# Expert weights in 8 KB rows and two experts per pass in the first expert stage of a two-block transformer kernel

## The chip, the cores and the metric

The kernel runs on one core of a Trainium2 chip (trn2). Its time is the device time of one execution in microseconds; the number that counts is the median of several executions. The core has TensorE (PE in the rows, with its weight loads as PEld), VectorE (DVE), ScalarE (ACT), GpSimd (POOL) and SyncE (SP), which here issues all DMAs; 16 DMA engines serve the core. TensorE's clock has two levels, 1.2 and 2.4 GHz; the profile shows the granted clock as a share of the higher one.

## The reference, cut to what matters

A first block (attention and feed-forward layers) is followed by a second block of two layers. Each of those two has attention branches and then a mixture of experts with 16 experts. In layer 0 the mixture runs over two streams of 256 tokens (`x` and the context), in layer 1 over `x` alone. Each expert takes the 32 tokens of a stream that score best for it, so 64 tokens in layer 0 and 32 in layer 1.

```python
def ec_moe(h, w_r, w1, w3, w2):
    B, n, D = h.shape
    cap = max(1, EC_CAPACITY * n // N_EXPERTS)          # 32
    aff = jax.nn.softmax((h @ w_r).astype(jnp.float32), axis=-1)
    gate, idx = lax.top_k(jnp.swapaxes(aff, 1, 2), cap)
    xin = jax.vmap(lambda hb, ib: hb[ib])(h, idx)
    hid = jax.nn.silu(jnp.einsum('becd,edf->becf', xin, w1)) * jnp.einsum('becd,edf->becf', xin, w3)
    ye = jnp.einsum('becf,efd->becd', hid, w2) * gate[..., None].astype(h.dtype)
    return jax.vmap(lambda yb, ib: jnp.zeros((n, D), h.dtype).at[ib.reshape(-1)].add(yb.reshape(-1, D)))(ye, idx)
```

Each of w1, w3 and w2 is 1024 x 1024 in fp32 for every expert, 12 MiB per expert and 192 MiB per layer.

## The kernel before

The program is written in the order of the model; a scheduler then orders the instructions of each engine, and pools of tiles set which buffer an instruction waits for. The expert part is the function `moe` (line 1540), called for layer 0 with two streams (`ns` = 2; "stage 0" below) and for layer 1 with one (`ns` = 1; "stage 1").

**Weights.** `ld` (line 1573) loads 256 rows of an expert's matrix, 1 MiB, into one tile of 8 KB per partition with `Ring.load` (lines 131 to 136). Partition p gets rows p and p + 128 of the 256, two runs of 4 KB. A `Ring` is a list of tile pools taken in turn, each of one tile: 16 tiles in stage 0 (lines 1546 and 1547), 19 in stage 1 (lines 1549 to 1551). A load waits on SP until the products that read the tile's last contents are done. SP issues DMAs in its own order, one after the other; what stands behind a waiting load waits too. Many of the ring's tiles lie where the attention part of the same layer had its buffers, so they come free as that part ends.

**First products** (`first_product`, lines 1576 to 1589). The gathered tokens `xin` are the stationary operand, the weights are the moving one, 512 columns at a time. In stage 0 the stationary operand has 64 columns, half of the array. Line 1585 multiplies by w1 into partitions 0 to 63 of a bank, line 1586 by w3 into partitions 64 to 127; the two run side by side. One expert takes two banks.

**Hidden layer and second products.** `gated` (line 1630) forms silu(a) * b on ScalarE and VectorE. `second_product` (line 1639) transposes it (line 1646), copies it to `hT` (line 1648) and multiplies by w2 (line 1655). With 64 tokens the contraction over 1024 is cut in two: the upper half of it goes to partitions 0 to 63 of `y`, the lower half to partitions 64 to 127, and the two are added by the scatter. The last expert's w2 comes in four slices of 256 columns, which have runs of 1 KB.

**Scatter.** For each quarter of the 1024 columns line 1686 scales `y` by the gate, lines 378 and 379 split it in two fp32r parts, lines 1693 and 1694 multiply a one-hot matrix `Se` by them for every 128 tokens, and line 1696 adds the result to the residual stream (`xr`, `xc`). This is done once per expert. In program order expert e's second products and scatter stand between the two halves of expert e + 1's first products.

**Start of a stage.** `u_gather` (line 1020) multiplies the normalised tokens by a one-hot matrix `G` to make `xin`, 128 features at a time, with the first expert's first products between. PSUM has eight banks, all from one pool.

Of the kernel before, what the change touches and what calls it, by code (L numbers as in the profile page):

```python
# [10 lines left out]
F32 = mybir.dt.float32  # L11
# [58 lines left out]
def model(ctx, tc, I, out):  # L70
# [6 lines left out]
    per = opool(ctx, "per")  # L77
    psum = opool(ctx, "psum", bufs=8, space=PSUM)
# [10 lines left out]
    def sub(hl, *ix):  # L89
        return hl[0][ix], hl[1][ix]  # L90

# [29 lines left out]
    class Ring:  # L121
# [9 lines left out]
        def load(self, src, k, c):  # L131
# [4 lines left out]
            return v  # L136

# [54 lines left out]
    pe.transpose(b[:, :128], rows, ident)  # L192
    dve.tensor_copy(cols, b[:, :128])

# [277 lines left out]
    def u_mod(ring, l, g):  # L472
# [22 lines left out]
        def fin():  # L495
# [3 lines left out]
            for q in range(4):  # L499
                pe.transpose(b2[:, q * 128:q * 128 + 128], mt[:, q * 128:q * 128 + 128], ident)  # L500
# [335 lines left out]
    for l in range(2):  # L836
        nc.sync.dma_start(WR[l], I["w_router_2"][l].rearrange("(k p) e -> p k e", p=128))
# [26 lines left out]
    def u_route(l, s, sp, half, pieces):  # L864
# [38 lines left out]
        def tr(t, i, on_act):  # L903
            def f():
# [4 lines left out]
                for k in range(c.start // 128, c.stop // 128):  # L909
                    pe.transpose(b[:, k * 128 - c.start:k * 128 - c.start + 128], X[s][:, t, k * 128:k * 128 + 128], ident)  # L910
# [109 lines left out]
    def u_gather(l, s, xs, engines):  # L1020
# [3 lines left out]
        def mm(c):  # L1024
            def f():
                b = banks[c] = bank("b")
                cs = slice(c % 4 * 128, c % 4 * 128 + 128)
                for t in range(2):
                    for i in range(2):
                        pe.matmul(b, xs[c // 4][i][:, t, cs], xs["G"][:, t], start=t == 0 and i == 0, stop=t == 1 and i == 1)  # L1030
            return f

        def ev(c):
            def f():
                bv = banks[c].rearrange("p (e c) -> p e c", c=32)
                if engines[c % 2] is act:
                    act.activation(xs["to"](c), bv, AF.Identity, scale=Amod[l][s][1][:, c:c + 1], bias=shiftcol(l, s, 1, c))
                else:
                    dve.tensor_scalar(xs["to"](c), bv, Amod[l][s][1][:, c:c + 1], shiftcol(l, s, 1, c), op0=ALU.mult, op1=ALU.add)
# [500 lines left out]
    def moe(l, ss, hp, sh, r, tail, ctx=None):  # L1540
# [3 lines left out]
        with ExitStack() as st:  # L1544
            if ns == 2:
                ring = Ring(st, f"rE{l}", 15, 0, [8, 9, 10, 11, 12, 13, 14, 0, 3, 1, 2, 4, 5, 6, 7])
                ring.ps.append(hp[1])
            else:
                ring = Ring(st, f"rE{l}", 17, 0, [0, 1, 2, 3, 4, 12, 13, 6, 5, 7, 8, 10, 9, 11, 14, 15, 16])
                ring.ps[0:0] = [late]  # L1550
                ring.ps[6:6] = [hp[1]]
            mo = opool(st, "mo", reuse_waits="tile")
            xin = mo.tile([128, 8, 16, ns, 32], F32, name="xin")
# [19 lines left out]
            def ld(w, i):  # L1573
                return ring.load(w[i * 256:i * 256 + 256], 2, 1024)

            def first_product(hb, e, i):
                t1, t3 = ld(I["w_e1_2"][l, e], i), ld(I["w_e3_2"][l, e], i)
                for kk in range(2):
                    k = 2 * i + kk
                    lhs = xin[:, k, e].rearrange("p s c -> p (s c)")  # L1580
                    fl = dict(start=k == 0, stop=k == 7, skip_group_check=True)
                    for n in range(2):
                        ns_ = slice(n * 512, n * 512 + 512)
                        if ns == 2:
                            pe.matmul(hb[n][0:64], lhs, t1[:, kk, ns_], **fl)  # L1585
                            pe.matmul(hb[n][64:128], lhs, t3[:, kk, ns_], **fl)  # L1586
                        else:
                            pe.matmul(hb[0][32 * n:32 * n + 32], lhs, t1[:, kk, ns_], **fl)  # L1588
                            pe.matmul(hb[0][64 + 32 * n:96 + 32 * n], lhs, t3[:, kk, ns_], **fl)  # L1589

            xs, px, pl = u_pieces(0, r, hp)
            xs["to"] = lambda c: xin[:, c, :, 0]
            gx, ex = u_gather(l, 0, xs, (dve, act))
            hb0 = [bank("h") for _ in range(ns)]
            if ns == 2:
                ctx["to"] = lambda c: xin[:, c, :, 1]
# [27 lines left out]
            dve.tensor_copy(rg, brg[:, 0:32])  # L1624
# [3 lines left out]
            gt = ap.tile([128, D], F32, name="gt")  # L1628

# [9 lines left out]
            def second_product(e, hd):  # L1639
# [5 lines left out]
                for c in range(4 * ns):  # L1645
                    pe.transpose(b[:, c * 64:c * 64 + 64], hd[64:128, c * 128:c * 128 + 128], ident[64:128, 64:128])
# [51 lines left out]
            gate_rows(ap, gt, l, 1, rowsel)  # L1698
# [57 lines left out]
```

## Time and profile before

| | |
|---|---|
| median of 3 runs | 2556.47 us |
| lowest and highest | 2555.18 and 2558.37 us |
| the profiled execution | 2554.91 us |
| its span, first to last instruction | 2553.2 us |
| TensorE busy, share of the span | 2393.4 us, 94% |
| VectorE | 1471.3 us, 58% |
| ScalarE | 1084.7 us, 42% |
| moved by DMA | 709.15 MB, mean 278 GB/s |
| mean granted TensorE clock | 0.990 |

The rows quoted further down are from that one profiled execution. A busy TensorE is not TensorE at its peak, since its matmuls overlap and their ends are modelled. A share over the whole span is an average over stages that differ; the stages are read one by one. Where a row says what an engine waited for, it names what ended the wait.

### The profile page before, as it was taken

Reading aid. Unit: us, or ns where it says so; the run is one execution under the profiler, and the core shown is the slowest. Engines: PE = TensorE matmul, PEld = TensorE weight load, DVE = VectorE, ACT = ScalarE, POOL = GpSimd, SP = SyncE. Lnnn points to the kernel's source line nnn. Section 1 sums busy time; section 2 is a strip of 40 time slices with the busy share of each in tenths; the row PEclk is TensorE's granted clock in tenths of the full one; section 3 lists DMA queues with packets and bytes.
Section 4 is the critical chain, followed back from the end, with each engine's and each line's share of the span. In section 5 each row is a group of like instructions: output and inputs, shape, how many; then the busy total and the mean of one; then the engine's idle time right before and its main releaser. Section 6 shows DMA issues by size and latency. Waiting matters only on the chain.

```text
span 2553.2 us, 39287 instructions
## 1 busy us (share of the span) xinstructions
PE 2393.4 (94%) x15290; PEld 1716.2 (67%) x15290; DVE 1471.3 (58%) x3033; ACT 1084.7 (42%) x2200; POOL 132.1 (5%) x188
## 2 busy tenths in 40 slices
PE   8999999999999999999999999998999989777776
PEld 7788979788998999799744444447879963222222
DVE  5687666687767877887633333436688663222223
ACT  5665555465666666565411111115656531000001
POOL 0100000010000100101200000001010000000000
PEclk9999999999999999999999999998999989999999
DMA  7477464577544455746699999995574779999998
GB/s 275 183 263 256 169 237 164 175 256 280 182 148 149 165 179 162 237 165 228 244 390 420 420 420 420 420 382 163 184 234 144 246 296 415 420 420 420 420 420 335
DMA packets 320491, 709.15 MB, mean 278 GB/s; under 512 B 28151, under 2 KB 178401, under 8 KB 314162
## 3 DMA queue, kind: packets, MB, share of 16 engines
q1 hardware_dynamic: 320306, 706.66, 74.0%
q8 instruction: 120, 1.97, 0.3%
q14 instruction: 65, 0.53, 0.1%
HBM read 705.49 MB, written 1.12 MB: 277 GB/s over the span
## 4 chain that ended last, share of the span: by engine, by line
PE 78%; DMA 12%; DVE 6%; ACT 2%; issue 1%; POOL 0%; SPq 0%; ACTq 0%; POOLq 0%; DVEq 0%
PE b L85 13%; PE b L87 13%; PE b L86 13%; DMA w<-in_w_e_dram 10%; PE h L1586 7%; PE y L1655 6%; PE acc L85 3%; PE acc L86 3%; PE h L1585 3%; PE acc L87 3%; PE b L1693 2%; PE b L1694 2%; PE h L1589 2%; PE b L491 1%; PE b L1172 1%
## 5 line engine op out<-in xcount | busy, mean ns | idle before, releaser
L148 DVE TENSOR_TENSOR wl<-w,wh 128x512 fp32r<-128x512 f32 x896 | 601.8, 696 | 191.0 <-ACT wh L146 150.2
L146 ACT ACTIVATE wh<-w 128x512 fp32r<-128x512 f32 x896 | 531.8, 627 | 220.2 <-PE b L86 115.2
L85 PE MATMUL b<-hTh,wh 128*128 128x256 f32 x1584 | 453.9, 287 | 6.4 <-ACT hTh L368 4.3
L86 PE MATMUL b<-hTl,wh 128*128 128x256 f32 x1584 | 447.6, 283 | 1.4 <-DVE hTl L359 1.4
L87 PE MATMUL b<-hTh,wl 128*128 128x256 f32 x1584 | 447.7, 283 | 0.0
L1686 DVE SCALAR_TENSOR_TENSOR yg<-y,rg,gt 128x256 f32<-128x256 f32 x128 | 56.3, 477 | 470.3 <-PE y L1655 469.9
L85 PEld LDWEIGHTS b<-hTh,wh 128*128 128x128 f32 x1584 | 300.2, 190 | 18.6 <-issue 5.7
L86 PEld LDWEIGHTS b<-hTl,wh 128*128 128x128 f32 x1584 | 299.7, 189 | 4.3 <-DVE hTl L359 1.8
L87 PEld LDWEIGHTS b<-hTh,wl 128*128 128x128 f32 x1584 | 300.0, 189 | 0.2 <-DVE wl L148 0.2
L1655 PE MATMUL y<-w,hT 128*64 128x512 f32 (+3 forms) x1088 | 268.3, 579 | 32.3 <-DMA w<-in_w_e_dram 29.8
L378 ACT ACTIVATE yh<-yg 128x256 fp32r<-128x256 f32 x128 | 51.8, 417 | 533.8 <-DVE yg L1686 527.4
L1585 PE MATMUL h<-w,xin 128*64 128x512 f32 x512 | 235.9, 600 | 0.0
L1586 PE MATMUL h<-w,xin 128*64 128x512 f32 x512 | 232.0, 598 | 0.0
L1655 PEld LDWEIGHTS y<-w,hT 128*64 128x64 f32 (+1 forms) x1088 | 80.3, 125 | 198.3 <-issue 134.2
L1588 PE MATMUL h<-w,xin 128*32 128x512 f32 x512 | 164.1, 610 | 10.0 <-DMA w<-in_w_e_dram 10.0
L87 PE MATMUL b<-hT,wl 128*128 128x256 f32 x560 | 156.3, 279 | 0.2 <-DVE wl L148 0.2
L85 PE MATMUL b<-hT,wh 128*128 128x256 f32 x560 | 156.4, 279 | 0.1
L86 PE MATMUL b<-hT,wh 128*128 128x256 f32 x560 | 156.1, 279 | 0.0
L1589 PE MATMUL h<-w,xin 128*32 128x512 f32 x512 | 123.2, 611 | 27.2 <-DMA w<-in_w_e_dram 27.2
L1586 PEld LDWEIGHTS h<-w,xin 128*64 128x64 f32 x512 | 65.5, 136 | 96.4 <-issue 90.4
L1693 PEld LDWEIGHTS b<-yh,Se 128*128 128x128 f32 x384 | 64.4, 189 | 90.0 <-ACT yh L378 71.3
L1693 PE MATMUL b<-yh,Se 128*128 128x256 f32 x384 | 93.6, 305 | 20.1 <-ACT yh L378 20.1
(377 smaller groups left out, 4306.8 us busy)
## 6 DMA issues: line engine op xcount, KB each, us to landing
w<-in_w_e_dram SPq DMA_DIRECT2D x384, 1024.0 KB
w<-in_w_in_dram SPq DMA_DIRECT2D x92, 1024.0 KB
w<-in_w_ada_dram SPq DMA_DIRECT2D x48, 1024.0 KB
w<-in_ffn_w_up_dram SPq DMA_DIRECT2D x44, 1024.0 KB
w<-in_ffn_w_down_dram SPq DMA_DIRECT2D x22, 1024.0 KB
w<-in_dil_w_qkv_dram SPq DMA_DIRECT2D x18, 1024.0 KB
w<-in_w_branch_dram SPq DMA_DIRECT2D x18, 1024.0 KB
w<-in_sb_w_qkv_dram SPq DMA_DIRECT2D x12, 1024.0 KB
```

Source lines behind the costliest of these rows:

```text
L85: pe.matmul(o, s[0], m[0], start=start, stop=False, skip_group_check=True)
L86: pe.matmul(o, s[0], m[1], start=False, stop=False, skip_group_check=True)
L87: pe.matmul(o, s[1], m[0], start=False, stop=stop, skip_group_check=True)
L146: act.activation(hi, part, AF.Copy)
L148: dve.tensor_tensor(lo, part, hi.bitcast(F32), op=ALU.subtract)
L1585: pe.matmul(hb[n][0:64], lhs, t1[:, kk, ns_], **fl)
L1586: pe.matmul(hb[n][64:128], lhs, t3[:, kk, ns_], **fl)
L1588: pe.matmul(hb[0][32 * n:32 * n + 32], lhs, t1[:, kk, ns_], **fl)
L1589: pe.matmul(hb[0][64 + 32 * n:96 + 32 * n], lhs, t3[:, kk, ns_], **fl)
L1655: pe.matmul(yb[cols.start // 512][M * q:M * q + M, cols.start % 512:(cols.stop - 1) % 512 + 1], hT[:, k], w, start=kk == 0, stop=last, ski ...
L1686: dve.scalar_tensor_tensor(yg[:, c_], yb[n][:, c_], rg[:, 16 + e:17 + e], gt[:, xs_], op0=ALU.mult, op1=ALU.mult)
L1693: pe.matmul(b[:, :256], lhs, yh, start=True, stop=False)
```

## The change

1. *Pairs of experts in stage 0.* `first_products` takes experts 2p and 2p + 1 together. The two halves of the array's columns hold the tokens of the two experts, the banks `h` are four (w1 in two, w3 in two). `pairs` holds the rest of the stage: `gated` works on 128 partitions, `turned` transposes 128 columns at a time and puts the result in place of the pair's `xin`, `second` multiplies the two experts' hidden layers by their own w2, each contraction whole in its half, and `added` scatters both experts at once. The scatter of pair p - 2 stands between the first products of pair p. The last pair's w2 comes in eight slices instead of four.
2. *Rows of 8 KB.* `load_pairs` puts rows 2p and 2p + 1 of the 256 on partition p, one run of 8 KB, in both stages. So row k of a product is now made of every second feature (`pair`). The gather, the router's and the hidden layer's transposes, the modulation columns (`cols`, through one more small load `rows2` at the start) and the router's weights are reordered to match.
3. *Two more weight tiles.* The DMA scratch in SBUF is set to 256 bytes, and two pools `early`, which exist from the start of the kernel, are put ahead of both rings: 18 and 21 tiles.

```diff
+    early = [opool(ctx, f"early{i}", reuse_waits="tile") for i in range(2)]
...
+    def pair(k, start=0):
+        o = k // 2 * 256 + k % 2 - start
+        return slice(o, o + 255, 2)
...
+        def load_pairs(self, src):
+            w = self.ps[self.at % len(self.ps)].tile([128, 2048], F32, name="w", tag="w8")
+            self.at += 1
+            nc.sync.dma_start(w, src.rearrange("(p k) c -> p (k c)", k=2))
+            return w.rearrange("p (k c) -> p k c", k=2)
...
+    rows2 = per.tile([128, 512], F32, name="rows2", tag="mt", bufs=1)[0:8, 0:256]
+    nc.sync.dma_start(rows2, I["g_norm2_2"].rearrange("l (i q) -> (l i) q", q=256))
...
-                    pe.transpose(b[:, k * 128 - c.start:k * 128 - c.start + 128], X[s][:, t, k * 128:k * 128 + 128], ident)
+                    pe.transpose(b[:, k * 128 - c.start:k * 128 - c.start + 128], X[s][:, t, pair(k)], ident)
...
-                        pe.matmul(b, xs[c // 4][i][:, t, cs], xs["G"][:, t], start=t == 0 and i == 0, stop=t == 1 and i == 1)
+                        pe.matmul(b, xs[c // 4][i][:, t, pair(c % 4)], xs["G"][:, t], start=t == 0 and i == 0, stop=t == 1 and i == 1)
...
                 ring.ps.append(hp[1])
+                ring.ps[0:0] = early
             else:
...
                 ring.ps[6:6] = [hp[1]]
+                ring.ps[0:0] = early
...
             def ld(w, i):
-                return ring.load(w[i * 256:i * 256 + 256], 2, 1024)
+                return ring.load_pairs(w[i * 256:i * 256 + 256])
+            def first_products(hb, p, i):
+                es = (2 * p, 2 * p + 1)
+                ts = [[ld(I[n][l, e], i) for e in es] for n in ("w_e1_2", "w_e3_2")]
+                for j in range(2):
+                    for kk in range(2):
+                        k = 2 * i + kk
+                        for n in range(2):
+                            for q in range(2):
+                                pe.matmul(hb[2 * j + n][64 * q:64 * q + 64], xin[:, p, k, q].rearrange("p s c -> p (s c)"),
+                                          ts[j][q][:, kk, n * 512:n * 512 + 512], start=k == 0, stop=k == 7, skip_group_check=True)
...
+            def pairs(hb):
...
+                def second(p):
+                    Se[p] = ap.tile([128, 512], F32R, name="Se", tag="Se", bufs=1)
+                    yb[p] = [bank("y") for _ in range(2)]
...
+                    if p < 7:
+                        for i in range(4):
+                            w = [ld(w2[q], i) for q in range(2)]
...
+                    else:
+                        for n in range(4):
+                            cols = slice(n * 256, n * 256 + 256)
+                            w = [ring.load(w2[q][:, cols], 8, 256) for q in range(2)]
...
+                hd = gated(hb)
+                for p in range(1, 8):
+                    hb = [bank("h") for _ in range(4)]
+                    for i in range(4):
+                        first_products(hb, p, i)
+                        if i == 0:
+                            turned(p - 1, hd)
+                        if p > 1:
+                            added(p - 2, i)
+                    hd = gated(hb)
+                    second(p - 1)
+                turned(7, hd)
+                for i in range(4):
+                    added(6, i)
+                second(7)
+                for i in range(4):
+                    added(7, i)
...
-    nc = _bacc.Bacc("TRN2", target_bir_lowering=False, num_devices=1)
+    nc = _bacc.Bacc("TRN2", target_bir_lowering=False, num_devices=1, dynamic_dma_scratch_size=256)
```

What the scheduler makes of it, at three places. A row is a source line, an operation, out<-in, the shape (for a matmul, stationary columns x moving columns) and a count.

SP's DMAs near the kernel's start, before; `w_ada` are the modulation weights, `gb` a norm gain, `sb_w_o` the first block's output weights:

```order
L135 DMA w<-in_w_ada_dram 128x2048 x3
L452 DMA gb<-in_norm_gains_dram 128x1024
L135 DMA w<-in_w_ada_dram 128x2048
L135 DMA w<-in_sb_w_o_dram 128x2x1024 x2
L135 DMA w<-in_w_ada_dram 128x2048
```

The same place after:

```order
L141 DMA w<-in_w_ada_dram 128x2048 x3
L470 DMA gb<-in_norm_gains_dram 128x1024
L148 DMA w<-in_w_e_2_dram 128x2048
L141 DMA w<-in_w_ada_dram 128x2048
L141 DMA w<-in_sb_w_o_dram 128x2x1024
L148 DMA w<-in_w_e_2_dram 128x2048
L141 DMA w<-in_sb_w_o_dram 128x2x1024
```

The first two loads of expert weights (`w_e`, one row of 2048 elements per partition) now stand here; the first two of stage 1 stand in the same way among the first weights of layer 1's attention.

TensorE within stage 0, from one expert's transposes (line 1646) on, before:

```order
L1646 MATMUL b<-ident,hd 128x64 x8
L1585 MATMUL h<-w,xin 64x512
L1655 MATMUL y<-w,hT 64x512 x16
L1586 MATMUL h<-w,xin 64x512
L1585 MATMUL h<-w,xin 64x512
L1693 MATMUL b<-yh,Se 128x256
L1694 MATMUL b<-yl,Se 128x256
```

The same work after, from the last first products of a pair on:

```order
L1607 MATMUL h<-w,xin 64x512 x40
L1697 MATMUL y<-w,xin 64x512 x32
L1607 MATMUL h<-w,xin 64x512 x10
L1688 MATMUL b<-ident,hd 128x128 x8
L1733 MATMUL b<-yh,Se 128x256
L1734 MATMUL b<-yl,Se 128x256
```

The second products are now those of the pair before, and the transposes and the scatter stand behind the first ten first products of the next pair but one.

TensorE at the end of stage 0, before, from the last slice of the last expert's w2:

```order
L1655 MATMUL y<-w,hT 64x256 x8
L1693 MATMUL b<-yh,Se 128x256
L1694 MATMUL b<-yl,Se 128x256
L1693 MATMUL b<-yh,Se 128x256
L1694 MATMUL b<-yl,Se 128x256
L1693 MATMUL b<-yh,Se 128x256 x4
L1694 MATMUL b<-yl,Se 128x256 x4
```

The same end after, from the third of four slices on:

```order
L1733 MATMUL b<-yh,Se 128x256
L1697 MATMUL y<-w,xin 64x256 x16
L1734 MATMUL b<-yl,Se 128x256
L1697 MATMUL y<-w,xin 64x256 x15
L1733 MATMUL b<-yh,Se 128x256 x6
L1734 MATMUL b<-yl,Se 128x256 x6
```

A slice is 16 matmuls instead of 8, and half of the last scatter stands ahead of the third slice's matmuls.

## Rows read from the trace of the kernel before

**Rows 1.** The page's slices: GB/s in 40 equal parts of the span.
```profile
GB/s 275 183 263 256 169 237 164 175 256 280 182 148 149 165 179 162 237 165 228 244 390 420 420 420 420 420 382 163 184 234 144 246 296 415 420 420 420 420 420 335
```

**Rows 2.** Stretches: us, busy per engine, granted clock, DMA share, GB/s.
```profile
1320.00:1700.00 380.00, 375.17 (x1802) 164.40 (x1800) 138.56 (x352) 44.74 (x92) 0.00 (x0) 1.00 1.03 420
2110.00:2530.00 420.00, 334.87 (x1766) 99.83 (x1768) 107.92 (x277) 41.94 (x94) 0.00 (x0) 0.99 1.03 420
```

**Rows 3.** Waits in 2110 to 2530 us: total us, times, longest.
```profile
PEld y L1655 <- DMA w<-in_w_e_dram: 55.7, 38, 3.0
```

**Rows 4.** Chain of work in stage 0: start us, us, what.
```profile
1299.52 6.87 PE y L1655 x32
...
1442.30 6.07 PE y L1655 x27
1449.40 0.74 PE b L1693 x4
1450.85 1.00 PE h L1585 x2
...
1471.07 6.07 PE y L1655 x27
```

**Rows 5.** Stretches where the loads of stage 0 and stage 1 end.
```profile
1718.00:1720.00 2.00, 2.00 (x12) 0.66 (x9) 0.00 (x0) 0.00 (x0) 0.00 (x0) 1.00 0.24 84
2538.00:2540.00 2.00, 1.65 (x20) 1.17 (x16) 1.18 (x4) 0.00 (x0) 0.00 (x0) 1.00 0.21 75
```

**Rows 6.** Timeline at the two stages' ends: start us, us, engine, line, operation.
```profile
1732.31 1.95 PE L1655 MATMUL y<-w,hT 128*64 128x256 f32 x16
...
1739.19 0.74 DVE L1696 TENSOR_TENSOR xr<-xr,b 128x256 f32<-128x256 f32 x2
...
2539.84 1.07 PE L1655 MATMUL y<-w,hT 128*32 128x256 f32 x16 [0.35 <-DMA w<-in_w_e_dram]
```

**Rows 7.** VectorE's groups, 1250 to 1740 us: count, busy, mean ns, idle before.
```profile
L1696 DVE TENSOR_TENSOR xr<-xr,b 128x256 f32<-128x256 f32 x128 | 47.9, 413 | 1.5 <-PE b L1694 1.2
L1686 DVE SCALAR_TENSOR_TENSOR yg<-y,rg,gt 128x256 f32<-128x256 f32 x64 | 28.3, 478 | 210.7 <-PE y L1655 210.4
L379 DVE TENSOR_TENSOR yl<-yg,yh 128x256 fp32r<-128x256 f32 x64 | 26.2, 424 | 6.1 <-ACT yh L378 4.7
```

**Rows 8.** The page's DMA packets by size, and the issues of w_ada.
```profile
DMA packets 320491, 709.15 MB, mean 278 GB/s; under 512 B 28151, under 2 KB 178401, under 8 KB 314162
...
w<-in_w_ada_dram SPq DMA_DIRECT2D x48, 1024.0 KB
```

**Rows 9.** SP's timeline, two issues: start us, us until issued, operation.
```profile
2.93 0.42 SPq L188 DMA_DIRECT2D rows<-in_g_norm_dram  x1
...
106.78 1.68 SPq L135 DMA_DIRECT2D w<-in_w_ada_dram  x3
```

**Rows 10.** Stretches of packets of 8, 8, 4 and 1 KB.
```profile
114.00:120.00 6.00, 6.00 (x47) 4.77 (x46) 2.63 (x6) 2.70 (x7) 2.13 (x2) 1.00 1.01 427
603.00:607.00 4.00, 4.00 (x26) 3.57 (x25) 3.31 (x7) 2.50 (x5) 0.00 (x0) 1.00 1.02 430
1480.00:1484.00 4.00, 4.00 (x20) 1.83 (x19) 3.49 (x10) 0.81 (x2) 0.00 (x0) 1.00 1.03 420
1708.00:1716.00 8.00, 7.77 (x45) 4.93 (x46) 7.20 (x21) 1.47 (x4) 0.00 (x0) 1.00 1.08 383
```

**Rows 11.** Stretches near the kernel's start and at layer 1's start.
```profile
70.00:80.00 10.00, 10.00 (x53) 7.53 (x51) 8.66 (x10) 7.89 (x12) 2.90 (x2) 1.00 0.03 11
1744.00:1752.00 8.00, 3.46 (x14) 2.92 (x14) 7.35 (x18) 6.20 (x16) 1.12 (x1) 0.71 0.00 0
```

**Rows 12.** Stretches at the start of stage 0.
```profile
1265.00:1270.00 5.00, 5.00 (x21) 1.96 (x19) 0.81 (x1) 0.78 (x1) 0.00 (x0) 0.86 0.01 3
1290.00:1300.00 10.00, 10.00 (x49) 3.41 (x49) 1.39 (x2) 2.66 (x5) 0.00 (x0) 1.00 0.87 323
```

**Rows 13.** TensorE's timeline, the first of stage 0's first products.
```profile
1266.62 0.64 PE L1585 MATMUL h<-w,xin 128*64 128x512 f32 x1
```

More of the change, by code (lines that the diff above doesn't have):

```diff
@@ L192, in model @@
     pe.transpose(b[:, :128], rows, ident)
+    for k in range(2):
+        pe.transpose(b[:, 128 + 8 * k:136 + 8 * k], rows2[:, pair(k)], ident[:8, :8])
     dve.tensor_copy(cols, b[:, :128])
+    dve.tensor_copy(cols[:, 80:96].rearrange("p (i k) -> p k i", k=2), b[:, 128:144].rearrange("p (k i) -> p k i", k=2))
     def prologue():
@@ L499, in fin @@
             for q in range(4):
-                pe.transpose(b2[:, q * 128:q * 128 + 128], mt[:, q * 128:q * 128 + 128], ident)
+                pe.transpose(b2[:, q * 128:q * 128 + 128], mt[:, pair(q) if g else slice(q * 128, q * 128 + 128)], ident)
             dve.tensor_copy(modT[l][:, g], b2.rearrange("p (b j r) -> p b j r", b=4, j=4)[:, :, :, 0:2])
@@ L1551, in moe @@
                 ring.ps[6:6] = [hp[1]]
+                ring.ps[0:0] = early
             mo = opool(st, "mo", reuse_waits="tile")
-            xin = mo.tile([128, 8, 16, ns, 32], F32, name="xin")
+            G = ns
+            xin = mo.tile([128, 16 // G, 8, G, ns, 32], F32, name="xin")
             rg = mo.tile([128, 32], F32, name="rg")
@@ L1579, in first_product @@
                     k = 2 * i + kk
[L1580 removed]
+                    lhs = xin[:, e, k, 0, 0]
                     fl = dict(start=k == 0, stop=k == 7, skip_group_check=True)
@@ L1583, in first_product @@
                         ns_ = slice(n * 512, n * 512 + 512)
[L1584 to L1589, printed above, removed]
+                        pe.matmul(hb[0][32 * n:32 * n + 32], lhs, t1[:, kk, ns_], **fl)
+                        pe.matmul(hb[0][64 + 32 * n:96 + 32 * n], lhs, t3[:, kk, ns_], **fl)
             xs, px, pl = u_pieces(0, r, hp)
-            xs["to"] = lambda c: xin[:, c, :, 0]
+            xs["to"] = lambda c: xin[:, :, c, :, 0]
             gx, ex = u_gather(l, 0, xs, (dve, act))
-            hb0 = [bank("h") for _ in range(ns)]
+            hb0 = [bank("h") for _ in range(4 if ns == 2 else 1)]
             if ns == 2:
-                ctx["to"] = lambda c: xin[:, c, :, 1]
+                ctx["to"] = lambda c: xin[:, :, c, :, 1]
                 gc, ec = ctx["gather"]
@@ L1623, in moe @@
                               ident[:16, :16], start=si == 0, stop=si == ns - 1, skip_group_check=True)
-            dve.tensor_copy(rg, brg[:, 0:32])
+            if ns == 2:
+                for q in range(2):
+                    r_ = slice(64 * q, 64 * q + 64)
+                    dve.tensor_copy(rg[r_, 0:16].rearrange("p (i g) -> p i g", i=2),
+                                    brg[r_, 0:32].rearrange("p (i g q) -> p i g q", i=2, q=2)[:, :, :, q])
+            else:
+                dve.tensor_copy(rg, brg[:, 0:32])
             rst.close()
@@ L1645, in second_product @@
                 for c in range(4 * ns):
-                    pe.transpose(b[:, c * 64:c * 64 + 64], hd[64:128, c * 128:c * 128 + 128], ident[64:128, 64:128])
+                    pe.transpose(b[:, c * 64:c * 64 + 64], hd[64:128, pair(c) if e < 15 else slice(c * 128, c * 128 + 128)],
+                             ident[64:128, 64:128])
                 if ns == 2:
@@ L1696, in second_product @@
                                 dve.tensor_tensor(x, x, b[:, :256], op=ALU.add)
-            gate_rows(ap, gt, l, 1, rowsel)
+            gate_rows(ap, gt, l, 1, rowsel, (lambda: per.tile([128, 512], F32, name="sel", tag="mt", bufs=1)) if ns == 2 else None)
+            if ns == 2:
+                return pairs(hb0)
             hd = gated(0, hb0)
```

63 lines of the change are left out of this document (58 added, 5 removed).

## The prediction

> **What bounds the kernel now.** I read the page's slices first, to find where DMA is level; then the stretches of time inside the two expert stages; then the waits and the chain of work there; and last the few microseconds at which each stage starts and ends. The slices show two plateaus of 420 GB/s, about 1276 to 1690 us and 2105 to 2550 us [rows 1]. These are the expert stages. Each moves 192 loads of 1.0486 MB, one load per 2.497 us at 420 GB/s.
>
> Over the plateaus DMA is at its cap in both stages, but TensorE is not in the same position [rows 2]. In stage 0 it is busy 375 of 380 us, in stage 1 only 335 of 420, and there it waits for expert weights (one of the lines: 55.7 us) [rows 3]. So stage 1 ends when its loads end. Stage 0 is nearly balanced: one expert takes TensorE 1471.07 - 1442.30 = 28.77 us [rows 4], while its 12 loads take DMA 12 x 2.497 = 29.96 us. TensorE started late and catches up on the lead that the 16 weight tiles give DMA. At the end of stage 0 the loads have all but stopped at 1718 to 1720 us, and TensorE's last products start only at 1732.31, the residual stream being complete at 1739.9 [rows 5, 6]. The last 20 us are TensorE's. After the change the question is therefore: how fast TensorE becomes, and when DMA then ends.
>
> **The change, part by part.** *Pairs of experts.* The first products do not change in number: before, the two halves of the array's columns held w1 and w3 of one expert, now they hold two experts. 16 matmuls of 512 columns took 6.87 us, 0.43 us each, with the halves overlapping [rows 4]. For two experts: 64 first products, 27.5 us; 32 second products, 13.7 us. The scatter back (lines 1693 to 1696) is what shrinks: before, each half held a partial sum of one expert and all of the scatter was done per expert; now one scatter serves two. One of its four pieces takes 1450.85 - 1449.40 = 1.45 us [rows 4], so 5.8 us per pair instead of 11.6. Transposes: 8 of 128 columns, taken as 1.6 us. Sum 48.6 us per pair against 57.5 before. DMA needs 24 loads per pair: 59.9 us at 420 GB/s. TensorE falls below DMA by 10 us per pair, so stage 0 becomes DMA's, and only part of the 8 x 8.9 = 71 us that TensorE saves reaches the end. VectorE's chain for one scatter is 16 x 0.414 + 4 x (0.478 + 0.42) = 10.2 us [rows 7]; with only two PSUM banks left beside the four of `h` and two of `y`, TensorE may be held to that pace, 53 us per pair, still below DMA.
>
> *Rows of 8 KB.* Expert weights now come as one run of 8 KB per partition instead of two of 4 KB. The trace of before has such runs: 48 loads of w_ada of 128 rows are 6144 of the 320491 - 314162 = 6329 packets that are 8 KB or more [rows 8]. Where several of those loads follow one another, as the three that SP issued from 106.78 us on [rows 9], DMA moved 427 and 430 GB/s; in stage 0 with its 4 KB packets 420, in its last loads of 1 KB packets 383 [rows 10]. I take 429, one load per 2.444 us. The ends for the range are 420 (no gain) and 431, just above the higher row.
> The Trainium skill weighs against this gain: "DMA: Bandwidth & Descriptors", section Specifications, gives 512 B as the smallest transfer for line rate, so by that page 4 KB and 8 KB rows would run alike. The rows differ from it (383, 420, 427 to 430 GB/s); by the page's rule the time would be that of rival B below.
>
> *Two more weight tiles.* `early` is ahead of both rings, so every load stands two tiles ahead of where it stood, until the ring has gone round. SP issues the first two of stage 0 near the kernel's start, right after a norm gain at about 66 us, where SP waited and DMA then moved 11 GB/s (70 to 80 us); the two of stage 1 at the start of layer 1, where DMA moved 0 GB/s (1744 to 1752 us) [rows 11]. No load waits behind them for a tile: these tiles have been idle or are freed by pair 6's second products. I take 1 us for loads that they push back, from 0 to 5.
>
> *Stage 0, when DMA ends.* The 16 tiles of before were full by 1265 us, when DMA moved 3 GB/s [rows 12]; now 18 loads are in by then, and 174 are left, 166 in 8 KB rows and the last 8 (before 4) in 1 KB pieces. The first first-product starts at 1266.62 [rows 13]; the first tiles come free after 8 matmuls, 3.4 us later, and DMA moves again about 1.5 us after that, at 1271.6 (the gap between last packets and first matmul at stage 1's end, as an estimate). From then four tiles come free in each 7 us of products and 2.1 us of gather, 2.3 us per tile, just faster than DMA. With such a thin backlog DMA moved 323 GB/s in 1290 to 1300 us [rows 12]; I take 3 us of loss for it. End of loads: 1271.6 + 166 x 2.444 + 8 x 2.74 + 3 = 1702.2 us, against about 1719.
>
> *Stage 0, what follows the last load.* Pair 6's weights are complete 8 x 2.74 = 22 us before that. TensorE is caught up there, but now has to do, in the written order, the scatter of pair 6 (10.2 us at VectorE's pace), 64 products of 256 columns (13.7 us) and two pieces of the next scatter between them (3 us); then the last two pieces, 5.7 us as before (1739.9 - 1734.26) [rows 6]. TensorE finishes pair 6's second products some 3.5 us after their weights, 18.5 us before the last load; 10.2 + 13.7 + 3 + 5.7 = 32.6 us of work from there end 14.1 us after it, and I take 14.5. Residual complete at 1702.2 + 14.5 = 1716.7 instead of 1739.9: **23.2 us**. Layer 1 then shifts as a whole.
>
> *Stage 1.* Its products keep their form, and DMA is its bound already. Two loads less in the plateau: 2 x 2.497 = 5.0 us. 167 loads at 2.444: 167 x 0.053 = 8.8 us. Together **13.8 us**, since the last loads end at 2538 to 2540, and the last matmuls wait for them [rows 5, 6].
>
> *Small things.* One more DMA (`rows2`, gains) stands ahead of the first weights on SP, 0.42 us for such a one [rows 9]. The stationary operands of gathers and of the router's and hidden transposes now step over every second element; no row of before has such a load, the nearest are the contiguous ones. Bounds: 0, as now, to twice the time, some 5 us per stage at the gathers; I take 0, since a gain has no reason and the next matmul mostly hides the load. The copies of `rg`, the selector tile and the router's weights are hidden by the loads in flight.
>
> **Sum.** 23.2 + 13.8 - 0.4 - 1 = 35.6 us. The profiled execution took 2554.91 us (span 2553.2), 1.6 below the median of 2556.47. 2556.5 - 35.6 = 2521; by the profiled execution 2519. I give 2520.
>
> **The rivals.** *B, the rows bring nothing:* the 8 KB rows run at 420 GB/s, say because the w_ada windows are too short to show a lasting rate. Stage 0's loads end at 1271.6 + 414.5 + 21.9 + 3 = 1711 us, which leaves 14.3 us; stage 1 keeps 5.0; less 1.4: 17.9 us, **2538**. For it: the windows are 4 and 6 us. Against it: the order 1, 4, 8 KB is monotonic.
>
> *C, TensorE still holds stage 0:* four banks for `h`, two for `y` and only two for transposes and scatter, with VectorE between, eat the 8.9 us per pair. Then stage 0 gains nothing and stage 1 its 13.8 - 1.4 = 12.4 us: **2544**. Against it: a pair has 10 us of slack.
>
> *D, the slower side: the clock.* TensorE now waits for weights in stage 0 too, and its granted clock, 1.00 there now, may fall in the waits. A pair takes 48.6/c us; over eight pairs the 12.4 us are used up when 48.6/c is 59 us, a mean clock below 0.82. At 0.75 it is 64.8 us, 58 us lost in the stage, and the kernel ends at about **2602**. Against it: stage 1 already waits like this, TensorE busy 80% of it, and was granted 0.99 [rows 2].
> The Trainium skill's "TensorE: Matmul & The Clock Gate", section HAM oscillation, describes such a loss where the wait for each slice is longer than its products; by that rule the time is D's, and stage 1's row speaks against it.
>
> *E, better:* the tail is shorter (its scatter hidden among the second products) and DMA runs at 431: 8 to 12 us more, **2509**.
>
> **How the numbers follow.** Forecast 0.58 (its own range 2512 to 2530), B 0.16, C 0.13, D 0.05, E 0.06, and 0.02 that the early loads or the stepped operands take nearly all. The range from 2507 to 2542 holds the forecast, B, most of E and some of C, about 0.8. Within 0.2% (5 us, about what a measurement of this kernel can tell from no change) lies next to nothing: faster 0.92, same 0.03, slower 0.05.
>
> **What would show it.** In stage 0: the plateau at about 429 GB/s, TensorE's busy share near 85% with waits on expert weights, a pair every 58.7 us, loads ending about 1702. In stage 1: two loads less and the same 429. A plateau at 420 means B; waits on VectorE or ScalarE at TensorE in stage 0 and DMA below its cap, C; a clock well under 1 there, D. I would be wrong altogether if the early loads were issued late, or if DMA idled while pairs hold four tiles at a time.

## The result and the profile after

| | before | after |
|---|---|---|
| median of 4 runs | 2555.82 us | 2520.68 us |
| lowest and highest | 2554.46 and 2558.37 us | 2520.26 and 2521.95 us |
| the profiled execution, and its span | 2554.91, 2553.2 us | 2520.92, 2519.2 us |

The ratio after to before is 0.9864, with an interval from 0.9848 to 0.9879. The prediction was 2520 us.

The page of the changed kernel: busy times, GB/s in 40 slices, packets, and the shares of the chain that ended last.

```profile
PE 2368.7 (94%) x15004; PEld 1706.3 (68%) x15004; DVE 1385.5 (55%) x2819; ACT 1062.6 (42%) x2152; POOL 132.1 (5%) x188
...
GB/s 273 216 259 260 183 218 176 160 245 268 217 151 155 159 168 168 220 151 235 251 372 427 427 427 427 427 414 227 189 232 151 227 303 400 427 427 427 426 427 343
DMA packets 274935, 709.11 MB, mean 281 GB/s; under 512 B 27135, under 2 KB 181489, under 8 KB 220994
...
PE 67%; DMA 26%; DVE 4%; ACT 1%; issue 1%; POOL 0%; POOLq 0%; SPq 0%; DVEq 0%; ACTq 0%
```

The two plateaus stand at 427 where [rows 1] has 420, and 53941 packets are now of 8 KB or more instead of 6329 [rows 8]. TensorE's share of the span is as before; only the chain tells that DMA now holds it for 26%. The same line of the page before:

```profile
PE 78%; DMA 12%; DVE 6%; ACT 2%; issue 1%; POOL 0%; SPq 0%; ACTq 0%; POOLq 0%; DVEq 0%
```

Stretches of the changed kernel, with the columns of [rows 2]: the plateaus, the restart of the loads in stage 0, their last 1 KB pieces, and the point where they end.

```profile
1290.00:1660.00 370.00, 361.31 (x1566) 151.09 (x1564) 67.53 (x172) 28.88 (x56) 0.00 (x0) 1.00 1.01 426
2110.00:2480.00 370.00, 300.39 (x1549) 90.51 (x1548) 93.62 (x238) 34.13 (x79) 0.00 (x0) 0.97 1.01 427
...
1269.00:1274.00 5.00, 5.00 (x26) 1.62 (x24) 0.00 (x0) 0.60 (x1) 0.00 (x0) 1.00 0.16 25
1274.00:1279.00 5.00, 5.00 (x24) 2.35 (x22) 0.81 (x1) 1.04 (x2) 0.00 (x0) 1.00 0.95 395
1279.00:1284.00 5.00, 5.00 (x26) 1.63 (x24) 1.42 (x2) 0.96 (x2) 0.00 (x0) 1.00 1.00 421
...
1684.00:1698.00 14.00, 10.83 (x68) 6.64 (x68) 9.17 (x25) 1.62 (x4) 0.00 (x0) 1.00 1.08 383
...
1708.00:1714.00 6.00, 5.45 (x47) 3.10 (x41) 0.94 (x3) 1.15 (x2) 0.00 (x0) 1.00 0.43 149
```

The chain of work through stage 0 (start us, us, what). Until 1433 us it consists of TensorE's products, from there to 1685 mostly of expert weights, and then of TensorE and VectorE in turn.

```profile
1420.62 12.83 PE h L1607 x59
1433.45 19.58 DMA w<-in_w_e_dram
...
1665.47 19.56 DMA w<-in_w_e_dram
1685.08 2.80 PE y L1697 x10
1687.91 0.49 DVE yg L1727
...
1695.73 7.08 PE y L1697 x64
...
1705.93 3.60 PE y L1697 x32
1709.85 3.61 PE y L1697 x30
```

The first of stage 0's first products on TensorE, VectorE's last addition to the residual, and the last slice's products of stage 1, in the timeline; the rows of before are [rows 13] and [rows 6].

```profile
1268.76 1.08 PE L1607 MATMUL h<-w,xin 128*64 128x512 f32 x4
...
1718.14 0.74 DVE L1736 TENSOR_TENSOR xr<-xr,b 128x256 f32<-128x256 f32 x2
...
2506.82 1.07 PE L1782 MATMUL y<-w,hT 128*32 128x256 f32 x16 [0.40 <-DMA w<-in_w_e_dram]
```

The residual is complete at 1718.9 instead of 1739.9 us, the last slice's products start at 2506.8 instead of 2539.8.

From the same rows of every profile taken, the span divides into four parts: the start of stage 0 (its first first-product), stage 0 up to the complete residual, layer 1's attention up to stage 1's first first-product, and the rest. All are in us; the experiments are told below.

| kernel | start of stage 0 | stage 0 | attention | stage 1 to the end | span | median |
|---|---|---|---|---|---|---|
| before | 1266.6 | 473.3 | 359.5 | 453.7 | 2553.2 | 2555.8 |
| after | 1268.8 | 450.1 | 358.3 | 442.0 | 2519.2 | 2520.7 |
| after2 (the same again) | 1267.3 | 453.5 | 359.4 | 442.5 | 2522.7 | 2521.0 |
| rows4 | 1265.7 | 457.6 | 358.7 | 449.6 | 2531.6 | 2532.9 |
| noearly | 1268.5 | 456.7 | 357.5 | 449.1 | 2531.8 | 2533.2 |
| onlypairs | 1268.8 | 462.0 | 357.6 | 453.7 | 2542.0 | 2542.6 |
| nopairs | 1268.6 | 475.9 | 356.6 | 441.7 | 2542.8 | 2544.2 |
| again1 | 1268.4 | 453.3 | 358.5 | 441.5 | 2521.7 | 2522.2 |
| again2 | 1268.9 | 468.5 | 358.6 | 441.5 | 2537.5 | 2540.0 |
| swap | 1268.2 | 447.2 | 359.1 | 441.6 | 2516.1 | 2518.6 |
| swap2k | 1264.0 | 445.6 | 357.4 | 441.0 | 2508.0 | 2516.4 |
| four | 1267.4 | 444.7 | 357.5 | 441.5 | 2511.0 | 2513.4 |

`after` and `after2` are one program; stage 0 differs by 3.4 us between their profiles. Single profiles therefore decide nothing below some 3 us in stage 0, and 1 us in stage 1. The runs were taken on several chips, and the median of the kernel before lay between 2555.8 and 2557.3 us beside them; differences of a microsecond or two between runs on different chips say little.

### The profile page after: what moved, and what is told of

Same layout as the page of the kernel before. It is cut to its first block, busy times and chain, and to the rows that moved or that the text cites. A ratio compares the mean times of both kernels' runs of the same rounds, so it can differ in the third digit from the quotient of the medians.

```text
span 2519.2 us, 38425 instructions
## 1 busy us (share of the span) xinstructions
PE 2368.7 (94%) x15004; PEld 1706.3 (68%) x15004; DVE 1385.5 (55%) x2819; ACT 1062.6 (42%) x2152; POOL 132.1 (5%) x188
## 4 chain that ended last, share of the span: by engine, by line
PE 67%; DMA 26%; DVE 4%; ACT 1%; issue 1%; POOL 0%; POOLq 0%; SPq 0%; DVEq 0%; ACTq 0%
DMA w<-in_w_e_dram 25%; PE b L86 13%; PE b L88 13%; PE b L87 13%; PE h L1607 5%; PE acc L86 3%; PE acc L87 3%; PE acc L88 3%; PE y L1697 2%; PE b L509 1%; PE b L1191 1%; DMA w<-in_w_ada_dram 1%; DVE wl L161 1%; PE b L1048 1%; PE o L1311 1%
## 5 line engine op out<-in xcount | busy, mean ns | idle before, releaser
L1607 PE MATMUL h<-w,xin 128*64 128x512 f32 x1024 | 257.9, 597 | 1.9 <-DMA w<-in_w_e_dram 1.9
L396 ACT ACTIVATE yh<-yg 128x256 fp32r<-128x256 f32 x96 | 39.1, 417 | 454.9 <-DVE yg L1813 268.9
L1607 PEld LDWEIGHTS h<-w,xin 128*64 128x64 f32 x1024 | 89.2, 136 | 145.5 <-issue 130.8
L1620 PE MATMUL h<-w,xin 128*32 128x512 f32 x512 | 168.8, 637 | 6.5 <-DMA w<-in_w_e_dram 5.5
L1813 DVE SCALAR_TENSOR_TENSOR yg<-y,rg,gt 128x256 f32<-128x256 f32 x64 | 28.1, 477 | 250.5 <-PE y L1782 250.3
L1782 PE MATMUL y<-w,hT 128*32 128x512 f32 (+1 forms) x544 | 130.4, 586 | 25.7 <-DMA w<-in_w_e_dram 25.2
L1621 PE MATMUL h<-w,xin 128*32 128x512 f32 x512 | 130.4, 640 | 21.1 <-DMA w<-in_w_e_dram 21.1
L1697 PE MATMUL y<-w,xin 128*64 128x512 f32 (+1 forms) x576 | 131.3, 551 | 7.9 <-DMA w<-in_w_e_dram 7.9
L1782 PEld LDWEIGHTS y<-w,hT 128*32 128x32 f32 x544 | 30.4, 111 | 122.1 <-issue 66.5
L1697 PEld LDWEIGHTS y<-w,xin 128*64 128x64 f32 x576 | 50.8, 136 | 82.0 <-issue 52.4
L88 PEld LDWEIGHTS b<-hT,wl 128*128 128x128 f32 x560 | 105.1, 188 | 0.4 <-DVE wl L161 0.4
```

The costliest lines, as they stand in the source:

```text
L88: pe.matmul(o, s[1], m[0], start=False, stop=stop, skip_group_check=True)
L396: act.activation(hi, src, AF.Copy)
L1607: pe.matmul(hb[2 * j + n][64 * q:64 * q + 64], xin[:, p, k, q].rearrange("p s c -> p (s c)"), ts[j][q][:, kk, n * 512:n * 512 + 512], star ...
L1697: pe.matmul(yb[p][cols.start // 512][64 * q:64 * q + 64, cols.start % 512:(cols.stop - 1) % 512 + 1], xin[:, p, k, :].rearrange("p q s c - ...
L1782: pe.matmul(yb[cols.start // 512][M * q:M * q + M, cols.start % 512:(cols.stop - 1) % 512 + 1], hT[:, k], w, start=kk == 0, stop=last, ski ...
L1813: dve.scalar_tensor_tensor(yg[:, c_], yb[n][:, c_], rg[:, 16 + e:17 + e], gt[:, xs_], op0=ALU.mult, op1=ALU.mult)
```

## The experiments

**rows4: runs of 4 KB again.**

```diff
 def pair(k, start=0):
-    o = k // 2 * 256 + k % 2 - start
-    return slice(o, o + 255, 2)
+    return slice(k * 128 - start, k * 128 - start + 128)
...
-    return ring.load_pairs(w[i * 256:i * 256 + 256])
+    return ring.load(w[i * 256:i * 256 + 256], 2, 1024)
```

> The changed kernel with expert weights in two runs of 4 KB per partition again; pairs and the two early tiles stay. Theory (the rows raise the rate of the loads, and both stages follow their loads): the plateaus go from 426 back to 420 GB/s, one load costs some 0.035 to 0.04 us more, so 166 loads of stage 0 about 6 us and 167 loads of stage 1 about 6.5 us: 12.5 us more, 2533 us. Rival B (the rows bring nothing, the rate has another cause): plateau stays at 426, 2521 us. If stage 0 were still held by TensorE, only stage 1 would lose: 2527 us.

Measured: 2532.86 us (2530.38 to 2533.91), 12.2 more than after. The same two stretches of rows4:

```profile
1290.00:1660.00 370.00, 359.94 (x1542) 147.21 (x1540) 67.60 (x172) 28.86 (x56) 0.00 (x0) 1.00 1.03 420
2110.00:2480.00 370.00, 291.83 (x1539) 86.59 (x1532) 95.80 (x246) 34.74 (x81) 0.00 (x0) 1.00 1.03 420
```

The loads differ from after's in the runs' length alone, and the plateaus fell to 420; with the runs the order of the features went back too, which changes TensorE's stationary operands and no load of expert weights. Each stage lost some 7.5 us by these profiles. Rival B is out.

**noearly: without the two early tiles.**

```diff
-                ring.ps[0:0] = early
```

(in both stages)

> The changed kernel without the two early tiles in the rings (16 and 19 tiles as before); pairs and rows of 8 KB stay. Theory (each early load is one load less in a plateau that DMA bounds): two loads of 2.46 us more per stage, 9.8 us, less up to 1 us that the early loads had pushed other loads back: 2529 to 2530.5 us. If stage 0 is TensorE's, only stage 1 loses: 2525.5 us. If the 2.2 us by which stage 0's first first-product now starts later come from the early loads, they go here (start back at 1266.6); if they come from TensorE's clock near 350 us (granted 0.61 in 350 to 353 us), the start moves with the clock there and not with the loads.

Measured: 2533.19 us (2530.57 to 2536.69), 12.5 more than after, some 3 us above what was expected: 6.6 us in stage 0, 7.1 in stage 1, where two loads are 4.9 each. Part of the rest can be seen at noearly's end: after a wait of 1.78 us for the last slice but one TensorE's 16 products of the last slice took 1.88 us instead of 1.07 (timeline), and over these 5 us it was granted 0.66 (stretch), so for a part of them the lower of its two levels.

```profile
2514.65 1.07 PE L1780 MATMUL y<-w,hT 128*32 128x256 f32 x16 [1.78 <-DMA w<-in_w_e_dram]
...
2517.53 1.88 PE L1780 MATMUL y<-w,hT 128*32 128x256 f32 x16
```

```profile
2515.00:2520.00 5.00, 4.41 (x40) 2.44 (x31) 2.19 (x6) 0.51 (x1) 0.00 (x0) 0.66 0.09 28
```

This chain and its scatter are 1.9 us longer than in after; the remainder, some 2 us, lies mostly in stage 0, within what single profiles differ by there, and stays open. The start of stage 0 did not come back with the loads (1268.5), and there was no dip of the clock near 350 us either, so neither of the two accounts of it holds for this profile; more on it in the last section.

**onlypairs: both of these undone.**

> Only the pairs of experts: rows of 4 KB and no early tiles, 16 and 19 tiles as before. Theory: rows and tiles add up, 12.5 + 9.5 us more than the changed kernel, 2543 us; against the kernel before this leaves some 13 us, all of it from stage 0 (its loads end at about 1717 us as before, but what follows the last load is 14 us instead of 21, and the tail of 20 us of TensorE's own work goes). Rival C (TensorE or VectorE still holds stage 0, pairs bring nothing): 2555 us.

Measured: 2542.63 us (2541.83 to 2544.07); ratio to before 0.9948, interval 0.9931 to 0.9964. Stage 1 is as before (453.7), and stage 0 is 11.3 us shorter. Rival C is out here too.

**nopairs: the loads of after, single experts.**

```diff
-            G = ns
+            G = 1
...
-                if ns == 2:
-                    return first_products(hb, e, i)
...
+                        if ns == 2:
+                            pe.matmul(hb[n][0:64], lhs, t1[:, kk, ns_], **fl)
+                            pe.matmul(hb[n][64:128], lhs, t3[:, kk, ns_], **fl)
...
-            if ns == 2:
-                return pairs(hb0)
```

> Rows of 8 KB and the two early tiles, but single experts in stage 0 (w1 and w3 in the two halves of the columns, as before). Theory (TensorE's 57.5 us per two experts against 59 of DMA bind stage 0): stage 0 gains nothing, its residual is complete at 1740 to 1742 us, and only stage 1 gains its 10.6 us: 2545 us (2543 to 2547). Rival (the loads alone made the gain, pairs are not needed): 2521 to 2526 us.

Measured: 2544.2 us (2543.67 to 2545.96); ratio to before 0.9956, interval 0.9939 to 0.9973. Its plateau, and then the end of its chain in stage 0:

```profile
1320.00:1700.00 380.00, 376.82 (x1792) 170.44 (x1790) 139.97 (x353) 45.94 (x94) 0.00 (x0) 1.00 1.01 426
```

```profile
1728.20 7.09 PE y L1778 x48
1736.91 1.90 PE y L1778 x16
```

DMA runs at 426 GB/s here, and stage 0 is no shorter than before (475.9 against 473.3): the loads are ready earlier, and TensorE's last products still start at 1737. Stage 1 has its whole gain of 12.0 us. Pairs alone bring 14.0 us, rows and tiles alone 12.4 (against 2556.6, before's median beside these runs), together 35.1 (after against its own before). The 8.7 us beyond the sum arise in stage 0: rows and tiles shorten it from 462.0 to 450.1 with pairs, and from 473.3 to 475.9, not at all, without.

**again1, again2: TensorE's slack in a pair, measured by filling it.**

```diff
-                            for kk in range(2):
+                            for kk in (0, 1) * 2 if i == 0 else (0, 1):
```

(again2: `* 3`)

> The changed kernel; in stage 0 the second products of pairs 0 to 6 do their first two of eight steps twice (8 products more per pair, 3.4 us of TensorE, the sums are started anew, so the result stays). Theory (stage 0 is DMA's; a pair takes TensorE 51.1 us where it runs without waits and DMA 59.0; TensorE starts some 25 us behind the loads and catches up 7.9 us per pair, until about 1433 us): with 54.5 us per pair it catches up 4.5 per pair, 25 us after 5.6 pairs, so still in time: 2521 to 2522.5 us. Rival C (TensorE still holds stage 0): 7 x 3.4 = 24 us more, 2545 us.

> The same with these two steps done three times (6.9 us of TensorE more per pair). Theory with the 51.1 us per pair of the trace: 58 us per pair, it catches up only 1 us per pair and is still some 18 us behind when the loads end: 2536 to 2540 us. If a pair took TensorE 48.6 us, as the prediction's sum had it: 55.5 us, 3.5 caught up per pair, the lead is gone at the end: 2521 to 2524 us. Rival C: 7 x 6.9 = 48 us more, 2569 us.

Measured: 2522.18 us (2520.04 to 2525.59) and 2539.96 us (2537.2 to 2540.63). The chain of again1 where TensorE catches up, and that of again2 late in stage 0:

```profile
1442.96 17.17 PE y L1697 x80
...
1497.46 17.17 PE y L1697 x80
...
1532.84 21.05 DMA w<-in_w_e_dram
```

```profile
1566.55 20.60 PE y L1697 x96
...
1624.49 20.60 PE y L1697 x96
...
1685.12 19.90 PE y L1697 x90
```

again1 takes 54.5 us per pair until it meets the loads at 1533 us instead of 1433, and ends as after does. again2 takes 57.9 and never meets them. Less the 3.4 and 6.9 us put in, a pair of after costs TensorE 51.1 and 51.0 us, and not 48.6; C would have been 24 and 48 us slower.

**swap: another order at stage 0's end.**

```diff
+                turned(6, hd)
+                for i in range(4):
+                    added(5, i)
+                second(6)
+                hb = [bank("h") for _ in range(4)]
+                for i in range(4):
+                    first_products(hb, 7, i)
+                    added(6, i)
+                turned(7, gated(hb))
+                second(7)
```

(the loop over pairs ends at 6)

> The changed kernel with another order at stage 0's end: pair 6's second products (and their loads) stand ahead of pair 7's first products instead of behind, so that pair 6's scatter runs among pair 7's first products and not between the last loads' products. Theory (after pair 6's second products TensorE has 31 us of its own work in the written order, the scatter of pair 6 with 9.2 us of VectorE among it, and this, not the loads, sets the end): the scatter's 9 us leave that chain, the last slice's load (ends at 1704.8 us) becomes the limit, 3.5 us of products and 5.4 us of scatter after it: residual complete at 1713 to 1715 instead of 1718.9, 2515 to 2517 us. Rival (the tail follows the last load already): 2521 us. Against it: if the later scatter of pair 5 or the new order of loads delays tiles, some us of it are lost.

Measured: 2518.55 us (2516.21 to 2520.29). TensorE now waits for the last slices:

```profile
1695.45 3.67 PE L1697 MATMUL y<-w,xin 128*64 128x256 f32 x32 [1.68 <-DMA w<-in_w_e_dram]
...
1706.32 3.67 PE L1697 MATMUL y<-w,xin 128*64 128x256 f32 x30 [0.33 <-DMA w<-in_w_e_dram]
```

The residual is complete 9.1 us after 1706.3. Against after, the time is 2.1 us less, with ranges that touch (3.6 us less when each is taken against the kernel before on its own chip): the direction fits, the size is below the 4 to 6 us expected. The last slice can be used only at 1706.3, some 1.5 us after the end of its packets as reckoned for after (1704.8, below).

**swap2k: the last weights in runs of 2 KB.**

```diff
-                        for n in range(4):
-                            cols = slice(n * 256, n * 256 + 256)
-                            w = [ring.load(w2[q][:, cols], 8, 256) for q in range(2)]
+                        for n in range(2):
+                            cols = slice(n * 512, n * 512 + 512)
+                            for h in range(2):
+                                w = [ring.load(w2[q][h * 512:h * 512 + 512, cols], 4, 512) for q in range(2)]
```

> As swap, and the last pair's second weights come as halves of 512 columns by halves of the rows (runs of 2 KB) instead of slices of 256 columns (1 KB). Theory (longer runs are faster, as between 1, 4 and 8 KB: 385, 420, 426 GB/s; 2 KB somewhere between, 400 to 415): the eight loads take 20.2 to 21 us instead of 21.8, the products and scatter after the last load stay 3.5 + 5.4 us: 1 to 1.6 us less than swap. Rival (512 B are enough for the full rate): the eight loads would already run at 426 in slices; they don't (385), and 2 KB would be as 1 KB: no change to swap.

Measured: 2516.44 us (2509.7 to 2518.99). The stretch of swap2k with 2 KB packets; after's 1 KB stretch stands above with 383:

```profile
1684.00:1698.00 14.00, 12.04 (x62) 5.41 (x62) 4.25 (x11) 2.00 (x4) 0.00 (x0) 1.00 1.05 408
```

The rate is where the theory has it. Stage 0 is 1.6 us shorter than in swap, which alone is inside the scatter. The profiled execution is 6.7 us below the median; its stage 0 started at 1264.0, some 4 us before that of swap, which is the larger part of it.

**four: four banks for the last pair, and after2 beside it.**

```diff
-                    yb[p] = [bank("y") for _ in range(2)]
+                    yb[p] = [bank("y") for _ in range(2 if p < 7 else 4)]
```

(with the last pair's products by quarters of 256 columns)

> As swap2k, and the last pair's products go into four PSUM banks of 256 columns instead of two of 512, so that VectorE can take up the third quarter of the columns while TensorE still multiplies for the last. Theory (what follows the last load is TensorE's 3.5 us of products and then a chain over VectorE and ScalarE for two quarters, 5.1 to 5.4 us): the first 1.4 us of that chain (gate, split) now lie beside the last quarter's products: from stage 0's first first-product to the complete residual 444.2 us instead of 445.6, time 2515 us (with stage 0 starting between 1264 and 1269 us: 2511 to 2517). Rival (the chain's length is set by VectorE's 8 additions at the end): no change to swap2k.

> The changed kernel again, beside the one above on the same chip. Both theories: 2520 to 2521 us. The start of stage 0 lies between 1264 and 1269 us in the profiles so far, with and without the early loads; if that is TensorE's clock after short waits, it scatters here too and the time with it.

Measured on one chip: four 2513.42 us (2512.69 to 2515.83), after2 2521.03 us (2519.84 to 2524.45). Against before, four has a ratio of 0.9836, interval 0.9822 to 0.9849; the times of four and after2 don't overlap. VectorE's first gate of the end now lies beside TensorE's last products, which end at 1707.9:

```profile
1706.24 0.48 DVE L1732 SCALAR_TENSOR_TENSOR yg<-y,rg,gt 128x256 f32<-128x256 f32 x1 [4.43 <-PE y L1717]
...
1711.34 0.74 DVE L1741 TENSOR_TENSOR xr<-xr,b 128x256 f32<-128x256 f32 x2
```

The residual is complete 4.2 us after the last product instead of 5.4. The three steps swap, swap2k and four together make 7.6 us, and four is the best version here. How the 7.6 us divide among the steps is not shown: the ranges of neighbouring steps overlap.

## Why the prediction was right, step by step

**TensorE falls below DMA in stage 0: right, its size off.** The step had 48.6 us per pair. Two pairs of after, one while TensorE holds the chain and one while DMA does, each from one pair's second products to the next:

```profile
1335.60:1386.70 51.10, 51.10 (x235) 21.61 (x233) 10.65 (x28) 3.93 (x8) 0.00 (x0) 1.00 1.01 426
...
1551.00:1610.00 59.00, 56.56 (x235) 23.03 (x233) 10.84 (x28) 3.92 (x8) 0.00 (x0) 1.00 1.01 427
```

The term that was mis-sized is the first products: 31.5 us instead of 27.5. The chain of work of the first of these pairs holds TensorE's products alone. A product of 512 columns shows as two records, so the 64 first products are 128 and the 32 second products 64:

```profile
1335.79 13.73 PE y L1697 x64
...
1356.41 3.58 PE h L1607 x12
...
1361.65 1.86 PE h L1607 x4
...
1369.55 17.37 PE h L1607 x80
```

The five pieces of first products take 5.14, 3.58, 1.86, 3.58 and 17.37 us. In the last, two records run side by side, 0.22 us for each of the 80. The other four stand between the pieces of the scatter and the transposes, and there some records of one half have none of the other half beside them: the four in 1.86 us take 0.47 each. rows4's chain has the same five pieces, so this is the scheduled order and not the loads. That leaves 51.1 - 13.7 (second products) - 31.5 - 1.2 (transposes) = 4.7 us for the scatter, less than the 5.8 of the sum. No piece of this chain is VectorE's: the 53 us given beside 48.6, for VectorE's pace, come near the number by another cause. The slack is 7.9 us per pair instead of 10; nothing hung on it, as again1 shows.

**TensorE's busy share near 85%: wrong, and it misleads.** The two stretches above have the same 235 records, and 51.1 against 56.6 us of busy time. Second products of the second pair, in the timeline:

```profile
1552.61 4.41 PE L1697 MATMUL y<-w,xin 128*64 128x512 f32 x16 [0.44 <-DMA w<-in_w_e_dram]
...
1557.53 4.34 PE L1697 MATMUL y<-w,xin 128*64 128x512 f32 x16 [0.51 <-DMA w<-in_w_e_dram]
```

Sixteen records take 4.4 and 4.3 us behind a wait for weights; in the first pair 64 took 13.7, 3.4 per sixteen. This fits loads of two experts that land one after the other: where one half's tile has come and the other's has not, records of one half run alone. The wait for weights thus shows in part as TensorE's work. The Trainium skill's "Perfetto Trace Analysis", section Identifying the Most-Contended Engine, says that the busy share of matmuls is a poor measure of how close TensorE is to its limit. The trace agrees: 96% in a pair with 7.9 us to spare.

**The rate: right in kind, too large in size.** 427 GB/s, not 429, and 420 without the rows. By SP's issues from load 247 to load 379, 132 loads went out in 330.6 us before and in 325.8 after, both in stage 1: 0.036 us less per load, where the step had 0.053.

**When stage 0's loads end: 1704.8 us, predicted 1702.2.** The eight slices and the two loads of layer 1 right behind them are ten loads in 1 KB pieces of 2.74 us. DMA falls off 2.3 us after 1708 (149 of 383 GB/s over 6 us), so the ten start at 1682.9 and the eighth ends at 1704.8. Four terms moved: the stage started 2.1 us later; the loads restart 5.7 us after the first product instead of 5.0; 166 loads took 408.5 us instead of 405.7; and the 3 us of thin backlog did not occur. That backlog was read from single experts [rows 12], and nopairs has it again (352 GB/s in 1290 to 1295 us); with pairs DMA is at 421 within 10 us of the restart. Without this cancelling the step would have missed by 5.6 us.

**What follows the last load: right.** Pair 6's second products are done 16.9 us before the last load (18.5 predicted), and 31.0 us of work follow them (32.6): complete 14.1 us after the load, 14.5 predicted. That this is the written order's price was the step's reason, and swap and four bear it out by taking part of it away.

**The stages and the sum.** Stage 0 became 23.2 us shorter in this profile, as predicted, and 19.8 in after2's: the agreement to the tenth is chance. The step's 23.2 was meant for the time at which the residual is complete, and that came 21.0 us earlier (1718.9 instead of 1739.9), since the stage started 2.1 us later. Stage 1 gained 11.7 (11.3 in after2) instead of 13.8: two loads at 2.5 us and 167 x 0.036 = 6.1 make 11.1. The profiled spans differ by 34.0 us and the medians by 35.1; the sum was 35.6.

**Small things.** The early loads cost nothing that can be seen: stage 0 starts at 1268.8 without them (onlypairs) and at 1265.7 with them (rows4). Loads of stepped stationary operands became longer: in the router's transposes from a median of 140 or 141 to 207 or 209 ns (48 of them), in the hidden layer's from 138 to 209 in stage 0 and 213 in stage 1 (64 each), in the gathers from 188 to 194 or 196 ns. With the contiguous operands of rows4 they are 138 to 141 ns in both kinds of transposes. Together that is some 12 us of load time in the kernel, an estimate from these rows, most of it beside running matmuls: the eight transposes of a pair take TensorE 1.16 us in after's chain and 1.02 in rows4's. How much of it reaches the end was not measured. At the gathers, where the bound was 5 us per stage, it is a fraction of a microsecond.

**The rivals.** B fell with rows4, C with again1 and onlypairs. E named what swap and four then took up, but not in the kernel as changed. D, the falling clock, did not come: granted 1.00 in 1290 to 1660 us, the higher level throughout (in stage 1's plateau 0.97, where before had 0.99). Waits in 1290 to 1660 us (total us, times, longest):

```profile
PEld y L1697 <- DMA w<-in_w_e_dram: 17.4, 15, 1.8
...
PEld h L1607 <- DMA w<-in_w_e_dram: 6.8, 8, 1.4
```

The Trainium skill's "TensorE: Matmul & The Clock Gate", section HAM oscillation, describes the loss for waits longer than the products between them. Here the two rows make 24 us of 370 and no wait is longer than 1.8 us, so this trace does not show that case.

## What to carry to other kernels

Before a load path is made faster, see whose chain the stage is: rows and tiles gave 0 in stage 0 while TensorE held it, and about 12 us once it didn't. TensorE's slack is measured by adding work until the time moves, not by its busy share. And when a stage becomes DMA's, its last 20 us are worth a look of their own: what stands in the written order behind the last load is exposed in full.

## What the runs showed of the hardware

- On this core the rate depends on the run's length far up: 383 GB/s at 1 KB, 408 at 2 KB, 420 at 4 KB, 427 at 8 KB. The Trainium skill's "DMA: Bandwidth & Descriptors", section Specifications, puts the least transfer for line rate at 512 B. These rows differ from it, and they decide.
- TensorE's granted clock differs between two executions of one program. after2 was at the lower level for most of a piece of the scatter at stage 0's end, and after was not. The same 18 records of matmuls in after2, and then in after:

```profile
1694.00:1697.50 3.50, 3.50 (x18) 3.27 (x20) 3.16 (x10) 0.34 (x1) 0.00 (x0) 0.56 1.08 376
```

```profile
1693.50:1695.80 2.30, 2.24 (x18) 2.11 (x20) 2.17 (x7) 0.40 (x2) 0.00 (x0) 1.00 1.07 374
```

The piece took 1.26 us longer (3.50 instead of 2.24) at a granted clock of 0.56 instead of 1.00.
- Near 350 us, behind an idle time of TensorE of 2.26 us, the clock falls in some profiles and not in others. Stretches of after, noearly and after2, in this order:

```profile
350.00:352.00 2.00, 2.00 (x14) 2.00 (x13) 1.85 (x5) 1.20 (x2) 0.53 (x1) 0.66 1.01 363
```

```profile
350.00:352.00 2.00, 2.00 (x18) 1.86 (x16) 1.85 (x4) 1.83 (x4) 0.52 (x1) 1.00 0.97 354
```

```profile
350.00:352.00 2.00, 2.00 (x12) 1.70 (x11) 2.00 (x4) 1.23 (x3) 0.00 (x0) 1.00 1.05 403
```

A mean of 0.66 over 2 us is the lower level, 1.2 GHz, for about two thirds of them. The dip comes with the early loads (after) and without them (onlypairs, 0.63), and is missing with them (after2) and without (noearly), so it is not theirs; which executions get it was not settled. Nor does this dip alone tell when stage 0 starts. TensorE's transposes just ahead of these stretches, in after and in after2:

```profile
349.36 0.75 PE L518 MATMUL b<-ident,mt 128*128 128x128 f32 x4 [2.26 <-DVE mt L515]
```

```profile
347.95 0.74 PE L518 MATMUL b<-ident,mt 128*128 128x128 f32 x4 [2.26 <-DVE mt L515]
```

From there to the start of stage 0 it takes some 919.4 us in both. after2 was granted 0.72 in 1247 to 1253 us instead, where after had 1.00. Whether such dips make the whole difference in that start, up to 4.9 us between the profiles, stays open.
